# New places for the temporaries of the block products of q and k, and the forget gate's sums behind the second block unit

## The chip, the cores and the metric

The kernel runs on one core of one Trainium2 chip. The metric is the device time of one execution in microseconds. Engines: PE is TensorE (matmuls), DVE is VectorE, ACT is ScalarE, POOL is GpSimd, SP is SyncE, which here only issues DMAs.

## The reference

One decoder layer on 1024 tokens of width 1024, all in float32:

```python
h = rms_norm(x, norm_mix_g)
proj = h @ w_in                       # q, k, v of two attentions, forget gate, branch gates
f_logit = fox_gate_columns + b_fgt
# dilated sliding-window attention (3 groups of 4 heads)          -> o_a
# forgetting attention (8 heads): logits q.k/8 + sum of log f     -> o_b
o_b = forgetting_attention(q, k, v, log_sigmoid(f_logit))
merged = g_a * (o_a @ w_dil_out) + g_b * (o_b @ w_fox_out)
x = x + merged @ w_out
# then a SwiGLU feed-forward block and a last rms_norm
```

The change lies in the projections to q and k, and in the small computation that turns the forget gate's logits into running sums of their log sigmoids.

## The kernel before

Every float32 operand of a matmul is held as a pair hi and lo of the reduced type fp32r. `split` (L96, L97) makes the pair: ACT copies to hi, DVE subtracts to get lo. A product is three matmuls: hi by hi, hi by lo, lo by hi.

The stages around the change, in order:

- *Values.* After the norm and the transposes (`hT_t`), the values of the two attentions are projected. In the pool "dilv" this stage holds two staging tiles `vst` (2 KB per partition each, stored to `vd_dram` by ACT's DMA queue) and the weights `w12` (hi and lo, 16 KB each). Meanwhile `form` prepares T1 to T4, combinations of blocks of `hT_t`.
- *Block units for q and k.* `projections` computes two column blocks of 128 weights at a time by a Strassen-like scheme: seven products of 12 matmuls (L287) with combined weights and combined inputs in place of eight. There are nine such units: four for the forgetting attention (the outer loop's `pr` of 0 and 2, q and k each), five for the dilated one. `left_side` prepares the weights of a unit: two raw tiles are loaded by SP (L254), POOL adds and subtracts them in four operations (L275 to L280) into `s` tiles, and `split` makes `A1`, `S12`, `S34` and `A22`. Then `prod` and the evacuations alternate: `cc` is the first bank copied by ACT (L313), `v2`, `v3` and the outputs `qo` come from joins on DVE (L318, L320). For the forgetting attention each output is split once more (`qh`) and hi and lo are stored to `fqk_dram`; for the dilated one `qo` is stored to `dqk_dram` from POOL's queue (L306).
- *The gate's sums.* `decay` takes the gate's logits `lf` through exp, Ln and a few small DVE operations (L520 to L530), two small matmuls with triangular and full ones (L534, L535), and DVE operations on their result (`tot`, `negc`). `negc` is first read by the logits of the attention.
- *Attention.* Score matmuls (L634, L635), ACT takes them out of the banks with `negc` as bias into the tiles `L` (L638), POOL masks the diagonal blocks (L641), DVE takes maxima, POOL reduces them over partitions (L649), DVE subtracts (L662), ACT takes the exp (L668). Beside it run two more plain projections (`ahead`, `pf` banks), to fill TensorE.

On each engine the order is that of a planner, which takes the program's order, the dependences and its own costs; `tc.issue_after(x)` puts the instructions of a block behind `x` on the engine of `x`, with no wait of its own.

Memory per partition is a stack of pools. The pool "proj" of the block units and, after it, the pool "attention" start at the place where "dilv" started. Within a pool, tiles lie in the order in which they are first asked for, a tag with as many places as it has buffers. With `reuse_waits="tile"` a tile waits for what still uses the earlier tiles at its place. In "proj" the gate's five tiles are asked for first, then the tiles of `projections` as they come. In "attention" come first

```python
R0 = apool.tile([P, 256], F32, name="R0", bufs=1)
R1 = apool.tile([P, 2, 256], F32, name="R1", bufs=1)
R2 = apool.tile([P, P], F32, name="R2", bufs=1)
```

(1, 2 and 0.5 KB), then the two `L` tiles of the first half of the queries (5 KB each).

Of the kernel before, what the change touches and what calls it, by code (L numbers as in the profile page):

```python
# [8 lines left out]
F32 = mybir.dt.float32  # L9
# [38 lines left out]
def layer_kernel(  # L48
# [53 lines left out]
        last_mm[0] = nc.tensor.matmul(psum, w.lo, m.hi, start=False, stop=stop)  # L102

    last_mm, last_hi, last_sq = [None], [None], [None]
    last_w = [None]

    def load_w(src, kt, n, tag="w", bufs=2, pool=None, chunk=None, rpool=None, rbufs=2, shared=0, between=None):

# [151 lines left out]
        split(w.hi[:], w.lo[:], raw)  # L260
        return w

    def left_side(pool, rg, ru, bufs, a22_bufs=2):
# [11 lines left out]
        nc.gpsimd.tensor_tensor(out=s12[:, :4], in0=u1, in1=u2, op=ALU.add)  # L275
        nc.gpsimd.tensor_tensor(out=s12[:, 4:], in0=s12[:, :4], in1=g1, op=ALU.subtract)  # L276
        S12 = fill(pair(KT, "s12", bufs), s12[:])
        s34 = pool.tile([P, KT, P], F32, tag="s", name=nm("s34"), bufs=2)
        nc.gpsimd.tensor_tensor(out=s34[:, :4], in0=g1, in1=u1, op=ALU.subtract)
        nc.gpsimd.tensor_tensor(out=s34[:, 4:], in0=g2, in1=s12[:, 4:], op=ALU.subtract)  # L280
        return A1, S12, fill(S34, s34[:]), fill(A22, u2)

    def prod(bank, a, b, first=False):
        for k in range(4):
# [2 lines left out]
                last_mm[0] = nc.tensor.matmul(bank[:], p, q, start=first and k == 0 and n == 0,  # L287
                                              stop=k == 3 and n == 2, skip_group_check=True)

    def projections(pool, T, c, dst, dls, sc, hl=False):  # L290

        T1, T2, T3, T4 = T

        def put(i, hh, op):

            st = pool.tile([P, dls[i], HALF // dls[i]], F32, tag="qo", name=nm("qo"), bufs=4)
            op(st[:], dls[i])
            if hl:
                flat = st[:].rearrange("p r i -> p (r i)")
                hi = pool.tile([P, HALF], F32R, tag="qh", name=nm("qh"), bufs=2)  # L300
                split(hi[:], flat, flat)
                d = dst[i][:, :, hh * HALF:(hh + 1) * HALF]
                nc.scalar.dma_start(out=d[0], in_=hi[:].bitcast(F32))
                nc.gpsimd.dma_start(out=d[1], in_=flat)
            else:
                nc.gpsimd.dma_start(out=residues(dst[i], dls[i], hh), in_=st[:])  # L306

        cc, v2, v3 = [pool.tile([P, HALF], F32, tag=n, name=nm(n), bufs=1) for n in ("cc", "v2", "v3")]
        A1, S12, S34, A22 = left_side(pool, *[raw_w(w_in[:, c0:c0 + P]) for c0 in c], 1)
        b1, b2, b3 = pd(), pd(), pd()  # L310

        def copy(out, bank, r=1):
            nc.scalar.activation(out=out, in_=view(bank[:], r), func=AF.Copy, scale=sc)  # L313

        def join(out, bank, other, r=1):
            p, q = view(bank[:], r), view(other[:], r)
            if sc == 1.0:
                nc.vector.tensor_tensor(out=out, in0=p, in1=q, op=ALU.add)  # L318
            else:
                nc.vector.scalar_tensor_tensor(out=out, in0=p, scalar=sc, in1=q, op0=ALU.mult, op1=ALU.add)  # L320

        flat = view(cc[:], 1), view(v2[:], 1), view(v3[:], 1)
        prod(b1, A1[:, :4], B11, True)
        copy(flat[0], b1)
        prod(b2, S12[:, 4:], T2, True)
        join(flat[1], b2, cc)
        prod(b1, A1[:, 4:], B21)
        put(0, 0, lambda o, r: copy(o, b1, r))
        prod(b2, S34[:, :4], T3)
        join(flat[2], b2, cc)  # L330
        prod(b3, S12[:, :4], T1, True)
        put(1, 1, lambda o, r: join(o, b3, v3, r))
# [179 lines left out]

    def decay(sums, az, u, t1, tot):

        nc.gpsimd.memset(sums[:], 1.0)
        nc.gpsimd.affine_select(out=sums[:, 0], in_=sums[:, 0], compare_op=ALU.is_ge, fill=0.0, base=0,
                                pattern=[[1, P]], channel_multiplier=-1)

        z = lf[:].rearrange("p a b -> p (a b)")
        nc.vector.tensor_scalar(out=t1[:], in0=z, scalar1=-1.0, scalar2=None, op0=ALU.mult)  # L520
        nc.vector.tensor_tensor(out=az[:], in0=z, in1=t1[:], op=ALU.min)
        nc.scalar.activation(out=az[:], in_=az[:], func=AF.Exp)
        nc.vector.tensor_scalar(out=u[:], in0=az[:], scalar1=1.0, scalar2=None, op0=ALU.add)
        nc.vector.tensor_scalar(out=t1[:], in0=u[:], scalar1=-1.0, scalar2=None, op0=ALU.add)
        nc.vector.tensor_tensor(out=az[:], in0=az[:], in1=t1[:], op=ALU.subtract)
# [18 lines left out]


    with pool_of("proj", 1) as upool:
        cums = [upool.tile([P] + d, F32, name=n, bufs=1) for n, d in (
            ("sums", [2, P]), ("az", [NT * 8]), ("u", [NT * 8]), ("t1", [NT * 8]), ("tot", [NT, 8]))]
        for pr in range(0, 4, 2):
            for a in range(2):  # L550
                c0 = FOX0 + a * FOX_W + pr * P
                projections(upool, T, (c0, c0 + P), [fqk_dram[a, pr + i] for i in range(2)], (1, 1),
                            (SCALE, 1.0)[a], True)
            if pr == 0:
                decay(*cums)
        for two in TWOS:
# [737 lines left out]
```

## Time and profile before

| | us |
|---|---|
| median of 3 runs (lowest to highest) | 1478.67 (1477.41 to 1481.15) |
| span of the profiled execution | 1476.9 |
| TensorE busy in it | 1442.2 |
| VectorE, ScalarE, GpSimd busy | 956.6, 558.0, 488.5 |
| granted TensorE clock, mean | 0.995 of full speed |

The profile is of one execution. Its span runs from the first to the last instruction; of its own time no more than that span is given, and it lies 1.8 us under the median of the runs. Timeline rows give start and duration in microseconds, engine, line, operation, output and inputs, their sizes, a count of merged instructions, and in brackets the idle time of the engine just before and what ended it. Rows of waits give the total, the number of times and the longest. A row of a DMA gives size and median time from issue to landing. `wh` and `wl` name all hi and lo weight tiles of the units, also `S12`; `s` is a tile of combined weights. Some matmul records can be missing from a trace.

### The profile page before, as it was taken

What the parts mean: (1) busy time and instruction counts of PE and PEld (TensorE: products, weight loads), DVE (VectorE), ACT (ScalarE), POOL (GpSimd) and SP (SyncE); (2) the same over time, 40 slices, a digit from 0 to 9 for tenths busy, and PEclk for the clock granted to TensorE, in tenths of its full rate; (3) what the DMA queues carried; (4) which work ended last, traced back from release to release, by engine and by line L of the source; (5) the groups of instructions that cost most, each with busy time, mean ns of one, the idle gap of its engine ahead of it and who ended that gap; (6) DMA issues with size and microseconds to landing.
All of it is one profiled execution on the core that took longest, in us unless ns stands there. A gap on an engine that the chain in (4) does not pass through costs nothing.

```text
span 1476.9 us, 18419 instructions
## 1 busy us (share of the span) xinstructions
PE 1442.2 (98%) x6876; PEld 1160.9 (79%) x6876; DVE 956.6 (65%) x1344; ACT 558.0 (38%) x832; POOL 488.5 (33%) x438
## 2 busy tenths in 40 slices
PE   8999999999999999999999989999999999999997
PEld 7897888787676676788888778888888887788886
DVE  6482654449889899836627865555566554876556
ACT  5342332236556423354315332232223323533333
POOL 1002434435433221110146146666666665000000
PEclk9999999999999999999999999999999999999999
DMA  8232444474534461275859232232333334976602
GB/s 229 72 107 71 147 160 126 131 214 123 134 108 114 154 209 43 65 240 160 305 199 341 101 86 79 93 106 95 107 107 107 105 104 135 326 250 214 183 31 100
DMA packets 165785, 213.58 MB, mean 145 GB/s; under 512 B 13760, under 2 KB 115136, under 8 KB 165440
## 3 DMA queue, kind: packets, MB, share of 16 engines
q1 hardware_dynamic: 129376, 119.06, 26.4%
q0 software_dynamic: 15200, 55.07, 10.5%
q10 hardware_dynamic: 21120, 38.28, 8.2%
q8 instruction: 54, 0.88, 0.3%
q14 instruction: 35, 0.29, 0.1%
HBM read 146.32 MB, written 66.06 MB: 144 GB/s over the span
## 4 chain that ended last, share of the span: by engine, by line
PE 79%; DVE 12%; issue 3%; ACT 2%; POOL 2%; DMA 1%; SPq 1%; DVEq 0%; POOLq 0%; ACTq 0%
PE pd L287 33%; PE pd L1211 10%; PE pd L100 6%; PE pd L102 6%; PE pd L101 6%; PE pf L102 3%; PE pf L100 3%; PE pf L101 3%; PE pd L197 2%; PE pd L193 2%; PE pd L194 2%; DVE wl L97 2%; PE pd L685 1%; DVE f L1120 1%; ACT wh L96 1%
## 5 line engine op out<-in xcount | busy, mean ns | idle before, releaser
L287 PE MATMUL pd<-hT_t,wh 128*128 128x512 f32 x856 | 264.9, 391 | 2.4 <-ACT cc L313 0.8
L287 PE MATMUL pd<-tT,wh 128*128 128x512 f32 x768 | 236.1, 389 | 4.0 <-ACT wh L96 4.0
L97 DVE TENSOR_TENSOR wl<-wr,wh 128x1024 fp32r<-128x1024 f32 (+2 forms) x110 | 130.7, 1189 | 134.4 <-ACT wh L96 134.2
L96 ACT ACTIVATE wh<-wr 128x1024 fp32r<-128x1024 f32 (+2 forms) x110 | 95.5, 868 | 277.9 <-PE pd L287 163.5
L287 PEld LDWEIGHTS pd<-hT_t,wh 128*128 128x128 f32 x856 | 159.9, 188 | 39.4 <-DVE sg L1011 4.2
L287 PEld LDWEIGHTS pd<-tT,wh 128*128 128x128 f32 x768 | 144.0, 188 | 34.7 <-ACT wh L96 4.9
L287 PE MATMUL pd<-hT_t,wl 128*128 128x512 f32 x428 | 166.6, 389 | 0.0
L287 PE MATMUL pd<-tT,wl 128*128 128x512 f32 x384 | 148.5, 390 | 0.1
L100 PE MATMUL pf<-hT_t,wh 128*128 128x512 f32 x288 | 114.2, 397 | 1.0 <-ACT wh L96 1.0
L102 PE MATMUL pf<-hT_t,wl 128*128 128x512 f32 x288 | 114.2, 397 | 0.0
L101 PE MATMUL pf<-hT_t,wh 128*128 128x512 f32 x288 | 114.1, 396 | 0.0
L96 ACT ACTIVATE wh<-s 128x1024 fp32r<-128x1024 f32 x58 | 61.5, 1060 | 117.5 <-POOL s L276 87.1
L97 DVE TENSOR_TENSOR ol<-raw,oh 128x1024 fp32r<-128x1024 f32 x64 | 77.3, 1224 | 43.7 <-ACT oh L96 40.3
L275 POOL TENSOR_TENSOR s<-wr 128x512 f32<-128x512 f32 x29 | 56.6, 1951 | 142.5 <-PE pd L101 65.0
L96 ACT ACTIVATE oh<-raw 128x1024 fp32r<-128x1024 f32 x64 | 67.2, 1068 | 91.9 <-PE pd L1211 83.5
L287 PEld LDWEIGHTS pd<-hT_t,wl 128*128 128x128 f32 x428 | 80.4, 188 | 16.7
L97 DVE TENSOR_TENSOR wl<-s,wh 128x1024 fp32r<-128x1024 f32 x58 | 75.4, 1299 | 24.1 <-ACT wh L96 24.0
L1211 PE MATMUL pd<-ol,oh 128*128 128x512 f32 x224 | 87.2, 389 | 0.0
L1211 PE MATMUL pd<-oh,ol 128*128 128x512 f32 x224 | 86.2, 389 | 0.0
L1211 PE MATMUL pd<-oh 128*128 128x512 f32 x224 | 85.2, 390 | 0.7 <-DVE acc L1182 0.7
L958 POOL TENSOR_TENSOR r<-r 128x512 f32<-128x512 f32 x32 | 43.1, 1359 | 124.9 <-DMA r<-in_w_ffn_down_dram 123.6
L287 PEld LDWEIGHTS pd<-tT,wl 128*128 128x128 f32 x384 | 72.1, 188 | 15.3 <-DVE wl L97 0.5
(278 smaller groups left out, 3065.0 us busy)
## 6 DMA issues: line engine op xcount, KB each, us to landing
wr<-in_w_in_dram SPq DMA_DIRECT2D x46, 512.0 KB, 4.4
wr<-in_w_ffn_in_dram SPq DMA_DIRECT2D x44, 512.0 KB, 3.9
raw<-left_dram SPq DMA_DIRECT2D x56, 256.0 KB, 3.9
g_dram<-fst ACTq DMA_DIRECT2D x32, 256.0 KB, 2.4
land<-g_dram SPq DMA_DIRECT2D x16, 512.0 KB, 3.5
r<-in_w_ffn_down_dram SPq DMA_DIRECT2D x8, 1024.0 KB, 10.7
right_dram<-r POOLq DMA_DIRECT2D x8, 1024.0 KB, 5.9
left_dram<-f POOLq DMA_DIRECT2D x8, 1024.0 KB, 4.7
```

Source lines behind the costliest of these rows:

```text
L96: last_hi[0] = nc.scalar.activation(out=hi, in_=src, func=AF.Copy)
L97: return nc.vector.tensor_tensor(out=lo, in0=src, in1=hi.bitcast(F32), op=ALU.subtract)
L100: nc.tensor.matmul(psum, w.hi, m.hi, start=start, stop=False)
L101: nc.tensor.matmul(psum, w.hi, m.lo, start=False, stop=False)
L102: last_mm[0] = nc.tensor.matmul(psum, w.lo, m.hi, start=False, stop=stop)
L193: nc.tensor.matmul(pt[hh][:], w.hi[:, k], m.hi, start=(k == 0), stop=False)
L194: nc.tensor.matmul(pt[hh][:], w.hi[:, k], m.lo, start=False, stop=False)
L197: nc.tensor.matmul(pt[hh][:], w.lo[:, k], m.hi, start=False, stop=(k == kt - 1))
L275: nc.gpsimd.tensor_tensor(out=s12[:, :4], in0=u1, in1=u2, op=ALU.add)
L287: last_mm[0] = nc.tensor.matmul(bank[:], p, q, start=first and k == 0 and n == 0, stop=k == 3 and n == 2, skip_group_check=True)
L958: nc.gpsimd.tensor_tensor(out=out, in0=p, in1=q, op=ALU.subtract)
L1211: nc.tensor.matmul(bank[:], p, q, start=new and n == 0 and i == 0, stop=n == last and i == 2, skip_group_check=True)
```

## The change

Three things:

1. `reserve` asks for tiles only to fix their places. In "proj" the output tiles `qo` and `qh` now come first, then the gate's tiles, then `cc`, `v2`, `v3`, `s34` and `a22`; `s` and `s12` follow as they are first used.
2. In the first unit alone, the splits of `S34` and `A22` and the copy to `cc` are put behind the hi half of `S12` on ACT.
3. In `decay`, the memset of `sums` is put behind the latest unit's last sum on POOL, and the exp behind the latest hi split on ACT. `decay` is called once, after the second unit, so these are the second unit's.

```diff
+    def reserve(pool, *places):
+        for tag, shape, dtype, bufs in places:
+            for _ in range(bufs):
+                pool.tile([P] + shape, dtype, tag=tag, name=nm(tag), bufs=bufs)
+
...
         S12 = fill(pair(KT, "s12", bufs), s12[:])
+        s12_hi[0] = last_hi[0]
...
-        nc.gpsimd.tensor_tensor(out=s34[:, 4:], in0=g2, in1=s12[:, 4:], op=ALU.subtract)
-        return A1, S12, fill(S34, s34[:]), fill(A22, u2)
+        last_s[0] = nc.gpsimd.tensor_tensor(out=s34[:, 4:], in0=g2, in1=s12[:, 4:], op=ALU.subtract)
+        with tc.issue_after(s12_hi[0].ins) if first else ExitStack():
+            return A1, S12, fill(S34, s34[:]), fill(A22, u2)
...
         prod(b1, A1[:, :4], B11, True)
-        copy(flat[0], b1)
+        with tc.issue_after(s12_hi[0].ins) if first else ExitStack():
+            copy(flat[0], b1)
...
-        nc.gpsimd.memset(sums[:], 1.0)
+        with tc.issue_after(last_s[0].ins):
+            nc.gpsimd.memset(sums[:], 1.0)
...
-        nc.scalar.activation(out=az[:], in_=az[:], func=AF.Exp)
+        with tc.issue_after(last_hi[0].ins):
+            nc.scalar.activation(out=az[:], in_=az[:], func=AF.Exp)
...
     with pool_of("proj", 1) as upool:
+        reserve(upool, ("qo", [HALF], F32, 4), ("qh", [HALF], F32R, 2))
         cums = [upool.tile([P] + d, F32, name=n, bufs=1) for n, d in (
             ("sums", [2, P]), ("az", [NT * 8]), ("u", [NT * 8]), ("t1", [NT * 8]), ("tot", [NT, 8]))]
+        reserve(upool, *[(t, [HALF], F32, 1) for t in ("cc", "v2", "v3")],
+                *[("s34" + n, [KT, P], F32R, 1) for n in "hl"], *[("a22" + n, [4, P], F32R, 2) for n in "hl"])
...
             projections(upool, T, (c0, c0 + P), [fqk_dram[a, pr + i] for i in range(2)], (1, 1),
-                            (SCALE, 1.0)[a], True)
+                            (SCALE, 1.0)[a], True, pr + a == 0)
```

More of the change, by code (lines that the diff above doesn't have):

```diff
@@ L104, in layer_kernel @@
     last_mm, last_hi, last_sq = [None], [None], [None]
-    last_w = [None]
+    last_w, last_s, s12_hi = [None], [None], [None]
     def load_w(src, kt, n, tag="w", bufs=2, pool=None, chunk=None, rpool=None, rbufs=2, shared=0, between=None):
@@ L261, in pair_of, with left_side @@
         return w
-    def left_side(pool, rg, ru, bufs, a22_bufs=2):
+    def reserve(pool, *places):
+        for tag, shape, dtype, bufs in places:
+            for _ in range(bufs):
+                pool.tile([P] + shape, dtype, tag=tag, name=nm(tag), bufs=bufs)
+    def left_side(pool, rg, ru, bufs, a22_bufs=2, first=False):
         def pair(k, tag, bufs):
@@ L288, in prod, with projections @@
                                               stop=k == 3 and n == 2, skip_group_check=True)
-    def projections(pool, T, c, dst, dls, sc, hl=False):
+    def projections(pool, T, c, dst, dls, sc, hl=False, first=False):
         T1, T2, T3, T4 = T
@@ L308, in projections @@
         cc, v2, v3 = [pool.tile([P, HALF], F32, tag=n, name=nm(n), bufs=1) for n in ("cc", "v2", "v3")]
-        A1, S12, S34, A22 = left_side(pool, *[raw_w(w_in[:, c0:c0 + P]) for c0 in c], 1)
+        A1, S12, S34, A22 = left_side(pool, *[raw_w(w_in[:, c0:c0 + P]) for c0 in c], 1, 2, first)
         b1, b2, b3 = pd(), pd(), pd()
```

## The prediction

> **What bounds the kernel now.** I read the page's busy shares first: they say which engine the sum has to be made on.
>
> ```profile
> span 1476.9 us, 18419 instructions
> PE 1442.2 (98%) x6876; PEld 1160.9 (79%) x6876; DVE 956.6 (65%) x1344; ACT 558.0 (38%) x832; POOL 488.5 (33%) x438
> ```
>
> TensorE is busy 1442.2 of 1476.9 us. Whatever takes no matmuls away, and this change takes none, can at best win back some of the other 34.7 us. So the next view is the waits of TensorE alone, for the stretch from just before the first block unit to the start of attention (118 to 330 us), and after it the busy time by stage:
>
> ```profile
> PE pd L287 <- ACT wh L96: 1.0, 1, 1.0
> PE pd L287 <- ACT cc L313: 0.8, 1, 0.8
> ...
> 133.50:154.00 20.50, 18.60 (x82) 14.50 (x81) 14.04 (x16) 8.83 (x13) 12.92 (x11) 1.00 0.44 129
> 154.00:173.00 19.00, 19.00 (x85) 15.72 (x85) 13.06 (x22) 6.94 (x10) 8.10 (x7) 1.00 0.42 132
> 173.00:192.00 19.00, 19.00 (x85) 15.73 (x85) 10.68 (x13) 6.21 (x10) 7.56 (x8) 1.00 0.47 154
> ```
>
> The columns are length, then busy us of PE, PEld, DVE, ACT and POOL, then the granted clock. Only the first unit has holes; the next two run without one. The two holes in the order of time (start, duration, what, idle before it):
>
> ```profile
> 133.08 0.39 PE L101 MATMUL pd<-wv,hT_t 128*128 128x512 f32 x1
> 133.31 0.39 PE L102 MATMUL pd<-wv,hT_t 128*128 128x512 f32 x1
> ...
> 136.03 0.39 PE L287 MATMUL pd<-hT_t,wl 128*128 128x512 f32 x1
> 137.23 0.73 PE L287 MATMUL pd<-hT_t,wh 128*128 128x512 f32 x2 [0.81 <-ACT cc L313]
> 137.80 0.40 PE L287 MATMUL pd<-hT_t,wl 128*128 128x512 f32 x1
> ...
> 139.86 0.39 PE L287 MATMUL pd<-hT_t,wl 128*128 128x512 f32 x1
> 141.27 1.19 PE L287 MATMUL pd<-tT,wh 128*128 128x512 f32 x4 [1.02 <-ACT wh L96]
> ...
> 142.87 0.63 PE L287 MATMUL pd<-tT,wh 128*128 128x512 f32 x2
> ```
>
> What stands behind each is in the chain of waits and in the other engines' timelines:
>
> ```profile
> 133.47 0.24 PE pd L102
> 133.74 0.61 ACT vst L501
> 134.36 2.14 DMA vd_dram<-vst
> ...
> 134.78 0.63 ACT L96 ACTIVATE wh<-wr 128x512 fp32r<-128x512 f32 x1 [0.44 <-ACT vst L501]
> 136.58 0.60 ACT L313 ACTIVATE cc<-pd 128x512 f32<-128x512 f32 x1 [1.17 <-DMA vd_dram<-vst]
> 137.08 0.25 ACT L522 ACTIVATE az<-az 128x64 f32<-128x64 f32 x1
> 140.18 1.04 ACT L96 ACTIVATE wh<-s 128x1024 fp32r<-128x1024 f32 x1
> ...
> 133.57 1.28 POOL L275 TENSOR_TENSOR s<-wr 128x512 f32<-128x512 f32 x1 [65.04 <-PE pd L101]
> 138.02 1.30 POOL L280 TENSOR_TENSOR s<-wr,s 128x512 f32<-128x512 f32 x1
> ...
> 79.65 2.35 SPq L254 DMA_DIRECT2D wr<-in_w_in_dram  x2
> ```
>
> The first hole: TensorE reuses the bank of the first product and needs `cc` copied out of it; that copy waits for the last store of `vst`, under which `cc` lies. The second: the hi half of `S12`. Its weights were ordered at 79.65 us, but POOL stood idle 65.04 us until TensorE let go of the memory of `s`, and then ACT took the forget gate's exp (137.08) and Ln before the split at 140.18.
>
> **The change part by part.**
>
> *The new places.* Sizes from the code, in KB from the pool's start: the value stage before it holds `vst` at 0-2 and 2-4, `w12` hi at 4-20 and lo at 20-36; beyond 36 nothing of that stage lies. Before: the gate's tiles 0-2, `cc` 2-4, `v2`, `v3` 4-8, `s34` 8-16, `a22` 16-24, `s` 24-32, `s12` 32-40, `qo` 40-48, `qh` 48-52. The two waits above fit it: `cc` on a `vst`, `s` on `w12`. After: `qo` 0-8, `qh` 8-12, the gate's tiles 12-14, `cc` 14-16, `v2`, `v3` 16-20, `s34` 20-28, `a22` 28-36, `s` 36-44, `s12` 44-52. So POOL's four sums and `S12`'s two splits need nothing of the value stage and can run once the weights are in, long before 133 us. DVE idles 20.58 us ahead of 131.29 us and takes the lo half there:
>
> ```profile
> 131.29 0.20 DVE L520 TENSOR_SCALAR t<-lf 128x64 f32<-128x64 f32 x1 [20.58 <-DMA vd_dram<-vst]
> ```
>
> `s34`, `a22` and `cc` still lie under `w12`, free at 133.7; ACT then has its `vst` copy (to 134.36), one split of 1.04 and one of 0.63, and the copy to `cc` at 136.3, when the first product ends. With `S12` ready, the program's own order can hold: 12 matmuls of `S12` with T2 (2.7 us at 0.227 each, the distance of the starts at 133.08, 133.31 and on to 136.03) cover that copy of 0.60.
>
> *Its gain.* Hole one: the stream would go on at 136.03 + 0.23 = 136.26, and starts at 137.23; the first three matmuls after it take 0.81 in place of 0.68. Together 1.10. Hole two: 139.86 + 0.23 = 140.09 to 141.27 is 1.18, and to 142.87 1.60 us where six matmuls take 1.36, so 0.24 more. Together 1.42, and the sum 2.5 us. Bounds: 1.8 (the two idle times alone, 0.81 + 1.02) and 2.8 (if the row x4 and its neighbour are five matmuls and none is missing). If the plan keeps the second product of the same bank right behind the first, some 0.7 of hole one stays (`cc` from 136.3 in place of 136.58). I take 2.5.
>
> *The gate's sums.* The exp now follows the last `qh` split of the second unit, the memset the second unit's last sum:
>
> ```profile
> 150.31 1.31 POOL L280 TENSOR_TENSOR s<-wr,s 128x512 f32<-128x512 f32 x1
> 163.86 0.61 ACT L96 ACTIVATE qh<-qo 128x512 fp32r<-128x512 f32 x1
> ...
> 138.13 1.27 DVE L525 TENSOR_TENSOR az<-az,t 128x64 f32<-128x64 f32 x1
> 140.61 0.23 DVE L530 SCALAR_TENSOR_TENSOR lf<-lf,az 128x64 f32<-128x64 f32 x1
> 153.53 0.33 PE L534 MATMUL pd<-lf,sums 128*128 128x64 f32 x2
> ```
>
> From exp (137.08) to L530's end is 3.8 us, now in the third unit, whose 19 us hold 10.68 us of DVE and 6.21 of ACT: there is room, and TensorE runs there without a hole. What is queued behind: on ACT the third unit's splits behind the exp of 0.25 us and a Ln like it, on DVE its splits and joins, on POOL the memset and the mask of `sums`, on TensorE all matmuls behind L534, which waited 12.7 us past its data before. What DVE makes of its result, `tot` and `negc`, moves along and is first read at 321.70. Price: 0 if L534 again stands late enough, up to 3.8 if it is placed the whole chain too early. I take 0. No DMA is added or moved past another. On SP's queue the second unit's weight loads follow the first unit's last reads of their two buffers, POOL's sums among them, and so come earlier, if at all changed.
>
> *The far end of the pool.* This is where I see a cost. Attention's first tiles lie over this pool: `R0`, `R1`, `R2` at 0-3.5 and the first logits `L` at 3.5-8.5. Before, that `L` lay over `v2`, and ACT waited for the last join that reads it; after, it lies over the last `qo`, and must wait until that is stored.
>
> ```profile
> 320.52 1.06 DVE L320 SCALAR_TENSOR_TENSOR qo<-pd,v 128x512 f32<-128x512 f32 x1 [1.57 <-PE pd L287]
> 321.70 2.95 ACT L638 ACTIVATE L<-pd,negc 128x512 f32<-128x512 f32 x6 [5.74 <-DVE qo L320]
> 321.88 0.90 POOL L306 DMA_DIRECT2D dqk_dram<-qo  x1 [1.75 <-DVE dl L598]
> dqk_dram<-qo POOLq DMA_DIRECT2D x1, 256.0 KB, 4.3
> DMA to landing us min/median/max: 3.0/4.3/7.3
> ...
> 325.95 0.39 PE L100 MATMUL pf<-hT_t,wh 128*128 128x512 f32 x1
> 326.48 0.58 POOL L641 TENSOR_SCALAR_AFFINE_SELECT L<-L 128x128 f32<-128x128 f32 x2
> 333.37 1.80 POOL L649 PARTITION_ALL_REDUCE mx<-mx  x1 [6.31 <-issue]
> 337.27 0.50 PE L634 MATMUL pd<-qx,kx 128*128 128x512 f32 x1 [1.48 <-ACT L L638]
> ```
>
> That store, issued at 321.88, lands 4.3 us later, at 326.2 (the row of landings is that of the five `qo` stores issued between 300 and 325 us). So the first L638 starts 4.5 us later than now. Six of them take 2.95 us, so they end at 329.2 where they ended at 324.65. POOL's masks ended at 327.06, 2.4 us behind them, since POOL makes the tables `R` in between; it can now do that while it waits, and ends one mask (0.29) behind, at 329.5. The all-reduce starts 6.31 us after that, at 335.8 where it was 333.37: 2.4 us later. TensorE has matmuls of the next projection to fill in, but already stands 1.48 us at 337.27 for the logits that ACT can't take before the exp of that all-reduce; what is late there is late in the end. Cost 2.4. Bounds: 0, if the plan puts other logits ahead on ACT so that TensorE finds work, and 4.5, if the whole delay passes through.
>
> [...]
>
> *Sum.* 1476.9 - 2.5 + 2.4 = 1476.8 us of span, a tenth under now. The profiled execution's span lies 1.8 under the median of the runs, 1478.67, and near their lowest, 1477.41; on the median's scale I say 1478.5. About 0.3% (4.4 us) is what a measurement of this kernel can tell from no change: its own three runs spread 3.7.
>
> **The rivals.**
>
> *The late store is hidden* (chance 0.27). The instruction order is planned; if the plan sees the store it can give ACT the second head's logits first (their memory, 8.5-13.5, was left long ago) and TensorE the 48 matmuls of the next projection. For it: those matmuls stand right behind, at 325.95. Against: the all-reduce of the first head still waits. Time: 1478.67 - 2.5, up to 0.5 of remaining cost: 1476.5.
>
> *Slower, by the late store* (0.16). The stores of that stretch are slow, up to 7.3 us. With a landing of L from issue, the first logits start L + 0.2 late; if the masks shrink no gap, that passes through whole. From L = 2.3 on, passed through whole, the gain of 2.5 is eaten; at 4.3 the kernel ends at 1478.67 - 2.5 + 4.5 = 1480.7, and at 7.3 at 1483.7. Against: the 2.4 us by which POOL now trails ACT are room for it.
>
> *The gate's matmuls stall TensorE* (0.06). L534 placed at the third unit's start would hold the queue up to 3.8 us; with the far end's 2.4 the time is up to 1482.4. Against: 12.7 us of margin before.
>
> *It doesn't do what it says* (0.05). If the plan still starts the first unit with two products of one bank and a late split, 1.8 us or so stay, and with 2.4 at the far end the time is 1480.4.
>
> *More than the holes* (0.06). With the late store hidden, a shifted plan could also take ACT's logits ahead of the exp and so close the 1.48 us at 337.27: 1478.67 - 2.8 - 1.5 = 1474.4, and less if others of TensorE's 34.7 us close too. Against: nothing in the edit aims there.
>
> **How the numbers follow.** The forecast has 0.40. Faster by over 0.3% (below 1474.2) needs the last rival with the scatter of the runs, and a little of the hidden store: 0.11. Slower (above 1483.1) needs the slow store passed through whole, or two costs together: 0.09. Within 0.3%: 0.80. The range reaches from a little under the hidden store with its best gain (1478.67 - 2.8 = 1475.9), less the 1.5 of the last rival and a little scatter, 1474, to the slow store at L near 6.5, 1483. The likeliest's own range, with the gain 1.8 to 2.8 and the cost a us to either side, 1.4 to 3.4, is 1477.3 to 1480.3.
>
> **What would show it.** Right: POOL's first L275 and `S12`'s split start before 120 us; TensorE's waits for `cc` and `wh` in the first unit are gone and its stream from 133.5 to 154 us is 2.5 us shorter; L522 comes after 160 us with no wait of TensorE at L534; the first L638 waits for a DMA of `qo` and TensorE's idle time near 337 us grows by what the all-reduce comes later. Wrong: no DMA named at L638 (the places at the far end are not as I worked out), a wait at L534, or holes between units where there were none.

## The result, and the profile after

| | before | after |
|---|---|---|
| median of 5 runs each, us | 1481.15 | 1496.97 |
| span of the profiled execution, us | 1476.9 | 1495.1 |
| granted TensorE clock, mean | 0.995 | 0.988 |

After over before is 1.0123, 95% interval 1.0108 to 1.0138. The changed kernel is slower by 1.23%, some 18 us, as are the profiled spans (18.2). The medians shown differ by 15.8 us: the ratio is not their quotient (1.0107). It is what the means give if only the three runs shown ahead count for the kernel before; with all five the means give 1.0111. The forecast was no change, with 1483 as its upper end, and it was wrong.

The same busy shares as before:

```profile
span 1495.1 us, 18414 instructions
PE 1451.3 (97%) x6876; PEld 1167.1 (78%) x6876; DVE 962.1 (64%) x1344; ACT 556.6 (37%) x832; POOL 494.5 (33%) x438
```

TensorE has the same 6876 matmuls, but 9.1 us more busy time and 9.1 us more idle time (43.8 for 34.7). Most of the idle part is in its waits from 118 to 350 us, in the new program's lines:

```profile
PE pd L544 <- DVE lf L540: 9.6, 1, 9.6
PE pd L647 <- ACT L L651: 3.3, 1, 3.3
PE pd L294 <- DVE v L325: 0.8, 1, 0.8
```

L544 is the first of the gate's two matmuls (L534 before), L647 and L651 are the score matmul and the logits (L634 and L638 before), L294 the unit matmul (L287 before). The first unit's two waits of before, 0.8 us for `cc` and 1.0 for `wh`, are gone; one of 0.36 for a `wh` stands at its last product. One wait of 9.6 us is new. The engines' timelines around it, first TensorE, then ACT, then DVE:

```profile
174.83 0.62 PE L294 MATMUL pd<-hT_t,wh 128*128 128x512 f32 x2
175.28 0.39 PE L294 MATMUL pd<-hT_t,wl 128*128 128x512 f32 x1
185.23 0.66 PE L544 MATMUL pd<-lf,sums 128*128 128x64 f32 x2 [9.56 <-DVE lf L540]
...
186.08 1.20 PE L294 MATMUL pd<-hT_t,wh 128*128 128x512 f32 x2
...
190.98 0.62 PE L294 MATMUL pd<-tT,wh 128*128 128x512 f32 x2
...
179.30 0.63 ACT L96 ACTIVATE qh<-qo 128x512 fp32r<-128x512 f32 x1 [1.53 <-DVE qo L325]
179.84 0.24 ACT L532 ACTIVATE az<-az 128x64 f32<-128x64 f32 x1
...
178.59 0.68 DVE L325 TENSOR_TENSOR qo<-pd,v 128x512 f32<-128x512 f32 x1
...
180.93 1.25 DVE L533 TENSOR_SCALAR u<-az 128x64 f32<-128x64 f32 x1
182.21 1.19 DVE L534 TENSOR_SCALAR t<-u 128x64 f32<-128x64 f32 x1
...
184.86 0.22 DVE L540 SCALAR_TENSOR_TENSOR lf<-lf,az 128x64 f32<-128x64 f32 x1
```

The gate's matmuls stand directly behind the last product of the second unit, which ends at 175.67. The exp stands behind the split of an output that is joined from that same product (join 178.59, split 179.30, exp 179.84), and `lf` comes 5.2 us after the exp starts. So TensorE waits 4.2 us for the exp to start and 5.2 for the chain behind it, with all later matmuls queued behind it.

Much of the added busy time is the clock. The 12 unit matmuls from 186.08 to 190.98 take 4.90 us, at full speed 2.72 (12 at 0.227, the distance of the starts at clock 1.00). The busy time by stretches says it too (length, busy us of PE, PEld, DVE, ACT, POOL, then the clock, the DMA share and GB/s):

```profile
180.00:185.00 5.00, 0.00 (x0) 0.00 (x0) 4.72 (x9) 0.34 (x2) 3.35 (x3) 0.53 0.63 198
185.00:190.00 5.00, 4.77 (x13) 4.00 (x14) 1.56 (x10) 0.00 (x0) 0.00 (x0) 0.50 0.62 169
190.00:195.00 5.00, 5.00 (x22) 4.07 (x21) 0.69 (x1) 0.60 (x1) 0.00 (x0) 0.95 0.00 0
```

The granted clock fell to half there (0.53, then 0.50). By the shares in the rows this began at 180.3 us, 4.6 us after the last matmul, and ended at 190.5, 5.3 us after the first one behind the gap.

Read in finer stretches, the clock in the traces is 1.00 or 0.50, nothing between, and outside the kernel's start and end each stretch at 0.50 lasts 3.4, 6.8 or 10.2 us. Before has one of 6.8 us between 100 and 1465 us (at 557.8); after has 10.2 at 180.3, 6.8 at 337.3 and 3.4 at 569.4 and 883.4. As an estimate, with half of TensorE's busy time inside these stretches lost, and the kernel's start counted, that is 11.5 us after and 5.1 before: 6.4 of the 9.1 us of added busy time.

The far end shows the wait that the prediction named there. In order: POOL's store and all-reduce, ACT's first logits, DVE's table, TensorE:

```profile
334.18 0.72 POOL L313 DMA_DIRECT2D dqk_dram<-qo  x1 [1.76 <-DVE dl L611]
349.05 1.80 POOL L662 PARTITION_ALL_REDUCE mx<-mx  x1 [6.18 <-issue]
...
338.44 2.83 ACT L651 ACTIVATE L<-pd,negc 128x512 f32<-128x512 f32 x6 [10.18 <-DMA dqk_dram<-qo]
...
337.35 0.43 DVE L617 CAST R<-dl 128x512 f32<-128x512 int32 x1 [2.87 <-DMA dqk_dram<-qo]
...
332.86 0.47 PE L647 MATMUL pd<-qx,kx 128*128 128x512 f32 x1
339.18 0.58 PE L647 MATMUL pd<-qx,kx 128*128 128x256 f32 x1 [3.32 <-ACT L L651]
353.98 0.50 PE L647 MATMUL pd<-qx,kx 128*128 128x512 f32 x1 [0.20 <-ACT L L651]
361.89 1.51 PE L698 MATMUL pd<-L,v 128*64 128x128 f32 x12
```

ACT waits for the store issued at 334.18 and starts 4.3 us later. TensorE's wait of before, 1.48 us some 16.4 us behind the first score matmul (337.27 - 320.85), is now 0.20 (at 353.98, 21.1 us behind it). The 3.32 us are a new wait, 6.3 us behind the first score matmul, for a bank that ACT has not yet emptied. From 337.3 on TensorE runs at half clock for 6.8 us, which before did not do there at all.

As a ledger, after minus before in the profiled executions, each a distance to the one event above it: the first unit starts 0.95 us later (the instructions of TensorE up to there are the same, so this is no part of the change; near 15 us this execution has 6.8 us at half clock and the one of before 3.4); its first 60 matmuls take 2.7 us less; from there to the first score matmul (320.85 before, 332.86 after) 13.7 us are lost, nearly all at the gate's matmuls; from there to the first values (345.42, 361.89) 4.5; to the end another 1.8.

### The profile page after: what moved, and what is told of

It is laid out like the page before. It is cut to its first block, busy times and chain, and to the rows that moved or that the text cites. A ratio compares the mean times of both kernels' runs of the same rounds, so it can differ in the third digit from the quotient of the medians.

```text
span 1495.1 us, 18414 instructions
## 1 busy us (share of the span) xinstructions
PE 1451.3 (97%) x6876; PEld 1167.1 (78%) x6876; DVE 962.1 (64%) x1344; ACT 556.6 (37%) x832; POOL 494.5 (33%) x438
## 4 chain that ended last, share of the span: by engine, by line
PE 78%; DVE 11%; DMA 4%; issue 2%; ACT 2%; POOL 2%; ACTq 0%; SPq 0%; DVEq 0%; POOLq 0%
PE pd L294 32%; PE pd L1224 10%; PE pd L100 5%; PE pd L101 5%; PE pd L102 5%; PE pf L102 3%; PE pf L100 3%; PE pf L101 3%; DVE wl L97 2%; PE pd L698 2%; PE pd L197 2%; PE pd L194 2%; PE pd L193 2%; DMA wr<-in_w_in_dram 1%; PE pd L647 1%
## 5 line engine op out<-in xcount | busy, mean ns | idle before, releaser
L294 PE MATMUL pd<-hT_t,wh 128*128 128x512 f32 x856 | 267.8, 395 | 1.6 <-ACT c L1093 0.7
L294 PE MATMUL pd<-tT,wh 128*128 128x512 f32 x768 | 235.6, 390 | 3.1 <-ACT wh L96 2.3
L294 PEld LDWEIGHTS pd<-hT_t,wh 128*128 128x128 f32 x856 | 161.9, 190 | 38.8 <-DVE sg L1024 4.2
L294 PEld LDWEIGHTS pd<-tT,wh 128*128 128x128 f32 x768 | 144.0, 188 | 34.1 <-ACT wh L96 3.1
L294 PE MATMUL pd<-hT_t,wl 128*128 128x512 f32 x428 | 167.8, 392 | 0.0
L294 PE MATMUL pd<-tT,wl 128*128 128x512 f32 x384 | 148.2, 390 | 0.5 <-DVE wl L97 0.5
L294 PEld LDWEIGHTS pd<-hT_t,wl 128*128 128x128 f32 x428 | 81.1, 190 | 17.1
L294 PEld LDWEIGHTS pd<-tT,wl 128*128 128x128 f32 x384 | 72.1, 188 | 16.2 <-DVE wl L97 1.4
```

## The experiments

Each is the changed kernel with one edit, unless it says otherwise. Ratios are against the kernel before, timed in the same session. The last three columns are changes of a distance against before, in us, from the profiled executions: "unit 1" from the first unit's first matmul to its 61st, "units" from there to the first score matmul, "far end" from there to the first values. "Half clock" is the time in the far end at which the granted clock was 0.50; before has none there. The profiles are of one execution each, so these columns hold whatever the clock did in it.

| kernel | ratio | 95% interval | unit 1 | units | far end | half clock |
|---|---|---|---|---|---|---|
| as changed | 1.0123 | 1.0108 to 1.0138 | -2.7 | +13.7 | +4.5 | 6.8 |
| no_gate_edges | 1.0057 | 1.0042 to 1.0073 | +0.5 | -0.6 | +4.7 | 6.8 |
| far_end_moved | 1.0105 | 1.0085 to 1.0125 | -2.7 | +13.3 | +2.1 | 3.4 |
| both | 1.0025 | 1.0013 to 1.0036 | +0.5 | -0.6 | +2.0 | 3.4 |
| gate_edges_alone | 1.0094 | 1.0076 to 1.0113 | -0.5 | +12.5 | +1.8 | 3.4 |
| warm_wait | 1.0095 | 1.0081 to 1.0110 | -2.7 | +11.4 | +6.2 | 6.8 |
| late_matmuls | 1.0045 | 1.0027 to 1.0062 | -2.7 | +5.6 | +2.6 | 3.4 |
| late_far | 1.0020 | 1.0010 to 1.0029 | -2.7 | +5.7 | -0.4 | 3.4 |
| mid_far | 1.0030 | 1.0017 to 1.0044 | -2.7 | +5.0 | 0.0 | 0 |
| gate_first | 1.0070 | 1.0058 to 1.0083 | -0.8 | -1.9 | +2.0 | 3.4 |
| gate_first_no_edges | 1.0045 | 1.0032 to 1.0059 | -0.1 | -2.0 | +2.1 | 3.4 |
| gate_split | 1.0012 | 1.0001 to 1.0022 | -1.2 | -0.6 | +1.0 | 0 |
| gate_split_ne | 1.0002 | 0.9990 to 1.0013 | -0.7 | -0.3 | +0.1 | 0 |
| gate_early | 1.0004 | 0.9995 to 1.0013 | -2.7 | +0.2 | +1.5 | 3.4 |
| gate_early_ne | 0.9991 | 0.9979 to 1.0003 | -0.7 | -0.3 | 0.0 | 0 |

### The two suspects, apart and together

no_gate_edges takes the two edges of `decay` away:

```diff
-        with tc.issue_after(last_s[0].ins):
-            nc.gpsimd.memset(sums[:], 1.0)
+        nc.gpsimd.memset(sums[:], 1.0)
...
-        with tc.issue_after(last_hi[0].ins):
-            nc.scalar.activation(out=az[:], in_=az[:], func=AF.Exp)
+        nc.scalar.activation(out=az[:], in_=az[:], func=AF.Exp)
```

> The change without its two edges in decay (memset behind the second unit's last sum, exp behind its last hi split); the new places and the first unit's edges stay. Theory, the gate's matmuls stand right behind the second unit's last product while exp waits for that product's own split: TensorE's wait of 9.6 us for lf and the slow matmuls behind it (some 2.4) go, so about 12 us under the changed kernel, some 5 to 6 over the kernel before (the wait for the stored qo stays). Rival, the new places disturb the second unit's loads and the edges only show it: within 2 us of the changed kernel.

far_end_moved asks for other tiles first in "attention", so that those that are written late lie where `qo` was:

```diff
+        reserve(apool, ("o", [HALF], F32, 2), ("den", [HALF], F32, 1), ("rc", [HALF], F32, 1))
```

> The change with attention's late tiles (o, den, rc, 8 KB) reserved first, so that they and not the tables R and the first logits L lie over qo. Theory: the first L651 no longer waits for the store of qo, TensorE's 3.3 us at its third-last score of the first group and the slow matmuls behind it (2.2) go: 5 to 6 us under the changed kernel, 12 to 13 over the kernel before. Rival, attention makes the delay up later (TensorE then waits elsewhere, at the all-reduce): under 2 us of difference.

The kernel "both" has both edits.

> Both of the above: no gate edges and attention's late tiles first. Theory: what stays is the first unit's gain, measured as 2.7 us in the changed kernel, so 1 to 4 us under the kernel before, ratio 0.997 to 0.999. Rival, the places cost something else in the units as well: at or over the kernel before.

gate_edges_alone is the kernel before with nothing but `decay`'s two edges:

```diff
+        with tc.issue_after(last_s[0].ins):
+            nc.gpsimd.memset(sums[:], 1.0)
...
+        with tc.issue_after(last_hi[0].ins):
+            nc.scalar.activation(out=az[:], in_=az[:], func=AF.Exp)
```

> The kernel before with the two edges of decay alone, old places, nothing at the first unit. Theory: the same wait at the gate's matmuls, 8 to 10 us and 2.4 of slow matmuls, so 10 to 13 us over the kernel before, less the part of the first unit's holes that exp and Ln made (under 1). Rival, places: within 2 us of the kernel before.

Measured: without the edges 1486.11 us where before is 1477.94, with the tiles moved 1492.45, with both 1482.15. All three fell short of their theory: no_gate_edges is 8.2 us over before and not 5 to 6, far_end_moved wins some 3 us on the changed kernel by the ratios and not 5 to 6, and "both" lies over before, where its rival had put it. Alone on the kernel before, the edges cost 1.0094, and TensorE's waits (118 to 350 us; the gate's lines of the kernel before have moved by 2) show the same number:

```profile
PE pd L536 <- DVE lf L532: 9.6, 1, 9.6
```

So the two edges of `decay` are the greater loss by themselves, with none of the new places. Without them, though, the first unit's gain goes as well. The waits of no_gate_edges:

```profile
PE pd L294 <- ACT wh L96: 3.0, 2, 2.8
```

With the gate's exp back in the first unit ACT comes to a split 2.8 us too late. The gain and the loss hang on the same edge: what is cleared out of the first unit has to go elsewhere.

At the far end the place of `qo` is worth 4.46 - 2.07 = 2.4 us with the edges and 4.65 - 2.01 = 2.6 without. Some 2 us remain, which gate_edges_alone (1.84) has too, with no new places; the last column says where most of them go. The far ends of far_end_moved, "both" and gate_edges_alone each hold 3.4 us at half clock, in which TensorE is busy for 3.0 to 3.4 us and so loses 1.5 to 1.7 by the estimate used above. mid_far, with the tiles moved and no half clock there, loses 0.0. And of the 2.4 to 2.6 for the place, some 1 us is the second 3.4 us at half clock and 0.9 to 1.2 idle time.

### The wait without the cold clock

warm_wait puts 33 small matmuls of constants, whose result is not used, behind the second unit's last product, ahead of the gate's matmuls:

```diff
+        for _ in range(33):
+            with tc.issue_after(last_mm[0].ins):
+                nc.tensor.matmul(pc[:, 128:256], ones[:], ones[:], start=True, stop=True)
```

> The changed kernel with 33 idle matmuls (ones by ones, 0.28 us each, 9.2 us in all, into the free part of the same bank) right ahead of the gate's two, so that TensorE is busy while lf is late; lf comes no earlier. Theory, the idle time itself lowers the granted clock: the clock stays at 1.00 between 175 and 195 us, the 12 matmuls behind the gate's take 2.7 in place of 4.9 us, and the kernel is about 2 us faster than the changed one. Rival, the slow matmuls have another cause (late weights): same time as the changed kernel or slower.

Its stretch from 180 us, where the changed kernel has 0.53:

```profile
180.00:185.00 5.00, 3.55 (x28) 3.06 (x27) 3.91 (x10) 0.26 (x1) 2.55 (x3) 1.00 0.63 171
```

The clock stays at 1.00 (a wait of 1.45 us for `lf` is left), and the first score matmul comes 2.3 us sooner than in the changed kernel (+11.4 for +13.7); the 12 unit matmuls behind the gap, slowed from 2.72 to 4.90 us, had said 2.2. So some 2.3 us of the loss are the clock, the rest the wait. At the far end this kernel loses 1.8 us more than the changed one, so its ratio doesn't show the 2.3 by itself.

### Giving the chain more time

late_matmuls moves the gate's matmuls and what follows them behind the third unit, late_far moves the tiles at the far end as well. mid_far puts the exp behind the first unit's last hi split, with the tiles moved:

```diff
+                if pr == 2 and a == 0:
+                    decay_sums(*cums)
```

```diff
-        with tc.issue_after(last_hi[0].ins):
+        with tc.issue_after(after_hi.ins):
...
+                if pr == 0 and a == 0:
+                    unit1_hi = last_hi[0]
```

> The change with the gate's two matmuls and what follows them (tot, negc) called one unit later, behind the third unit; the exp stays behind the second unit's last split. Theory, the stall is the place of the two matmuls in TensorE's queue: lf is ready some 10 us before they are reached, the wait of 9.6 us and the slow matmuls are gone and the first unit keeps its gain of 2.7: 11 to 14 us under the changed kernel, 2 to 5 over the kernel before (the far end's wait stays). Rival, it is the gate's small operations, late on ACT and DVE, that hold up the next unit's splits wherever the matmuls stand: a wait of several us for wh or wl in the third unit, under 6 us won.

> The late matmuls, and attention's late tiles reserved first. Theory: the first unit's gain without either cost: 1 to 4 us under the kernel before, ratio 0.997 to 0.999. Rival, the gain is given back in attention, as the kernel with both edges out and the tiles moved did: within 1 us of the kernel before or over it.

> The change with the exp behind the first unit's last split instead of the second's (the matmuls stay behind the second unit in the program), and attention's late tiles first. Theory: lf is ready near 170 us, before the second unit's last product ends at 175.7, so no wait at the gate's matmuls, while the first unit keeps its gain: 1 to 4 us under the kernel before. Rival, the exp's place matters less than its lateness anywhere behind the first unit: a wait for lf of over 2 us stays.

The 9.6 us are gone in all three, but none reaches the kernel before, and 5.0 to 5.7 us are still lost in the units. TensorE's waits in late_matmuls, and then its DVE and POOL:

```profile
PE pd L294 <- DVE v L327: 2.4, 1, 2.4
...
184.09 1.29 DVE L533 TENSOR_SCALAR u<-az 128x64 f32<-128x64 f32 x1
185.41 1.21 DVE L534 TENSOR_SCALAR t<-u 128x64 f32<-128x64 f32 x1
...
188.06 0.68 DVE L327 SCALAR_TENSOR_TENSOR v<-pd,cc 128x512 f32<-128x512 f32 x1
...
183.66 1.67 POOL L285 TENSOR_TENSOR s<-wr,wr 128x512 f32<-128x512 f32 x1 [1.95 <-DVE wl L97]
185.29 1.28 POOL L286 TENSOR_TENSOR s<-wr,s 128x512 f32<-128x512 f32 x1
```

The gate's small operations now stand on DVE ahead of the joins (`v`) that TensorE needs, and hold them by 2.4 us (2.7 in mid_far). Each of the first two ends with an addition of POOL (183.66 + 1.67 = 185.33, 185.29 + 1.28 = 186.57). The clock falls after that too, for 3.4 us from 189.6 on:

```profile
189.70:192.90 3.20, 3.20 (x9) 2.51 (x8) 1.92 (x2) 1.50 (x2) 0.54 (x1) 0.50 1.10 391
```

That costs another 1.7 us by the same estimate, behind a wait of 2.4 that ended at 188.8; the changed kernel's was 9.6. What lowers the clock isn't shown here. The wait and the clock are 4.1 of the 5.6 us; a wait of 1.9 us for the load of `qx`, just ahead of the first score matmul (0.4 before), is most of the rest.

### The gate's work ahead of the units

gate_first calls `decay` ahead of the first unit, without its two edges, with its temporaries past 36 KB and `sums` and `tot` at the pool's start; `qo` moves to 27 to 35 KB, away from the far end's tiles. gate_first_no_edges also drops the first unit's edges.

```diff
+        sums = upool.tile([P, 2, P], F32, name="sums", bufs=1)
+        tot = upool.tile([P, NT, 8], F32, name="tot", bufs=1)
+        reserve(upool, ("qh", [HALF], F32R, 2), ...
+        reserve(upool, ("qo", [HALF], F32, 4), ("pad", [192], F32, 1), ("s", [KT, P], F32, 2),
...
+        decay(sums, az, u, t1, tot)
...
-            if pr == 0:
-                decay(*cums)
```

> The gate's sums ahead of all block units instead of behind two of them: decay is called before the loop, its three small tiles lie behind everything the value stage still uses, sums over the earlier vst, its edges are gone. qo lies at 27-35 KB, so the tables and the first logits of attention no longer lie over it. The first unit's edges stay. Theory: the gate's small operations run in the stretch where DVE and ACT stand idle (111 to 131 us) and cost nothing there; the first unit keeps its 2.7 us, there is no hole in the second and third unit and no wait for the store of qo: 1 to 4 us under the kernel before, ratio 0.997 to 0.999. Rival, the first unit's gain is always paid back in attention: within 1 us of the kernel before or over it.

> The same without the first unit's two edges (copy to cc and the splits of S34 and A22 behind the hi half of S12). Theory: with the gate out of the way and S12 ready early the edges bind nothing, so the same time within 1 us and no new hole in the first unit. Rival, they are what keeps the order of ACT right: a wait for cc or wh of 1 us or more comes back in the first unit.

```profile
PE pd L542 <- POOL sums L524: 7.6, 1, 7.6
...
131.77 0.31 POOL L523 MEMSET sums<- 128x256 f32 x1 [62.76 <-DMA vd_dram<-vst]
138.96 1.25 POOL L280 TENSOR_TENSOR s<-wr 128x512 f32<-128x512 f32 x1 [6.88 <-issue]
```

`sums` lay over a `vst`, so its memset waited until 131.77, and on POOL everything stands behind it, the first unit's sums too. Then POOL's first addition came 6.88 us late with no releaser named, and TensorE stood 7.6 us for `sums`, ahead of the first unit, which began at 142.61 us and had 3.9 us at half clock in it. That was a fault of this experiment's places, not an answer. gate_first_no_edges has the same stall (8.2 us), and no wait came back in its first unit. It was expected within 1 us of gate_first and came out 4.05 us faster; in the profiles that lies behind the first values, and its cause isn't shown.

gate_split keeps these places but leaves the memset (with its edge), the mask, the matmuls and what follows them (`decay_sums`) behind the second unit; only exp to `lf` come first, without an edge. gate_split_ne drops the first unit's edges.

```diff
+        decay(az, u, t1)
...
             if pr == 0:
-                decay(*cums)
+                decay_sums(sums, tot)
```

> The gate's elementwise work (exp to lf) is done ahead of the first unit, in memory past 36 KB, where its inputs don't wait for the value stage; its memset, mask, matmuls, tot and negc stand behind the second unit, with none of the two edges of the changed kernel; qh, v2, v3 and not qo lie under attention's first tiles. My theory (what is lost is lost by the gate's small operations between TensorE's joins and by an idle TensorE that then runs at a lower granted clock, and the far end's loss is the place of qo): no wait of TensorE for lf or sums of more than 0.5 us, no wait of the first logits for a store of qo, the first unit's stream 2.0 to 2.8 us shorter than before, and a ratio of 0.998 to 1.000 (1475.5 to 1478.5 us where before is 1478.7). Rival one, that the first unit's gain is always given back by the units behind it, whatever the gate does, because their weights, sums and splits are no earlier: a ratio of 1.000 to 1.002, with the gain seen at the 60th unit matmul and gone at the 120th. Rival two, that ACT's exp and Ln ahead of the first unit delay the copies of the value stage and so the start of the first unit: the start is 0.5 to 1.5 us later and the ratio 1.000 to 1.002.

> The same without the first unit's edges (splits of S34 and A22 and the copy of the first bank behind the hi half of S12). My theory: with the gate's work gone from the first unit the planner's own order serves, and the result is that of the kernel with those edges within 1 us, a ratio of 0.998 to 1.000. Rival: without those edges ACT takes a late split before an early one, TensorE waits up to 1.5 us for cc or wh in the first unit, and the ratio is 1.000 to 1.001.

No stall at the gate's matmuls, no wait for a store, and ratios of 1.0012 and 1.0002. But ACT's order in gate_split, with TensorE's wait:

```profile
138.43 1.20 PE L294 MATMUL pd<-tT,wh 128*128 128x512 f32 x4 [1.21 <-ACT wh L96]
...
135.58 0.26 ACT L526 ACTIVATE az<-az 128x64 f32<-128x64 f32 x1 [0.44 <-ACT vst L509]
137.18 0.26 ACT L532 ACTIVATE u<-u 128x64 f32<-128x64 f32 x1 [1.34 <-DVE t L530]
137.34 1.04 ACT L96 ACTIVATE wh<-s 128x1024 fp32r<-128x1024 f32 x1
```

The exp and the Ln still came behind the last copy of `vst` and ahead of the split, although their input had been ready 19 us. The theory expected 2.0 to 2.8 us at the first unit and got 1.2, and both ratios lie over the 0.998 to 1.000 expected.

gate_early therefore writes exp to `lf` into the value stage, between two copies of `vst`, over the weights `w0` that are no longer needed; gate_early_ne again drops the first unit's edges.

```diff
+                if (g0, tt) == (1, 5):
+                    w0_ctx.__exit__(None, None, None)
+                    with pool_of("gate", 1, side="right") as gpool:
+                        decay(*[gpool.tile([P, NT * 8], F32, name=n_, bufs=1) for n_ in ("az", "u", "t1")])
...
+        with tc.issue_after(last_st[0].ins):
+            nc.scalar.activation(out=az[:], in_=az[:], func=AF.Exp)
```

> As the kernel with the gate's work split, but the elementwise part (exp to lf) stands inside the value stage, between two copies of vst on ACT, in three small tiles over the weights that the value stage no longer needs; the sums and matmuls behind the second unit, the first unit's edges kept. My theory: what held the first unit's splits in that kernel (TensorE 1.21 us idle for the hi half of S12, behind exp and Ln on ACT at 135.58 and 137.18 us) is gone, the first unit's stream is 2.5 to 2.8 us shorter than before (distance from the first to the 60th unit matmul 13.6 to 13.9 us where it was 16.37), the gate's matmuls wait for nothing, and the ratio is 0.997 to 0.9995 (1474.2 to 1478.2 us where before is 1478.98). Rival: the gain is there at the 60th unit matmul, but the units behind it and the attention give it back, since their order is replanned and their waits are others; then no single wait over 1 us is named and the ratio is 1.000 to 1.002.

> The same without the first unit's edges. ACT then takes the copy of the first bank ahead of the hi half of S12. My theory: TensorE waits 0.5 to 0.9 us for cc in the first unit and 0 to 0.6 for a join behind it, so 0.7 to 1.5 us more than with the edges there, and the ratio is 0.998 to 1.000. Rival: the edges do nothing once the gate is out of the way; the first unit is within 0.3 us of that with them.

gate_early, the stretches of the first three units (the first of these rows starts 1 us ahead of the unit, which begins at 134.53); they answer to the three rows of before in the prediction:

```profile
133.50:154.00 20.50, 20.35 (x90) 16.32 (x89) 11.45 (x11) 8.52 (x12) 8.54 (x8) 1.00 0.39 115
154.00:173.00 19.00, 19.00 (x87) 15.71 (x86) 12.45 (x20) 7.13 (x10) 7.50 (x7) 1.00 0.42 136
173.00:192.00 19.00, 19.00 (x86) 15.73 (x85) 10.01 (x13) 7.02 (x10) 7.08 (x7) 1.00 0.47 159
```

Here is the whole gain: the first unit 2.7 us shorter, no wait of TensorE for a unit's data, and the first score matmul still 2.45 us closer to the first unit's start than before. Yet the time is 1478.74 us where before is 1478.07. gate_early_ne has two waits in the first unit:

```profile
137.13 0.74 PE L294 MATMUL pd<-hT_t,wh 128*128 128x512 f32 x2 [0.69 <-ACT cc L320]
149.27 0.74 PE L294 MATMUL pd<-tT,wh 128*128 128x512 f32 x2 [0.97 <-DVE v L327]
```

It reaches the first score matmul only 0.94 us sooner, 1.5 us behind gate_early, and ends ahead of it: 1476.52 us. It is the best kernel found, some 20 us faster than the changed one, but against before its interval (0.9979 to 1.0003) includes no difference. The two differ in the first unit's edges alone. Between the first score matmul and the end of the attention (the matmuls with `oh` and `wh`, at 649.5 us before) gate_early loses 1.2 us against before and gate_early_ne wins 1.9, with TensorE's instructions in another order there, though neither edits that part. So the rival of gate_early's expectation was right about the ratio and the place, though a wait of 2.2 us is named there and not none over 1 us. What the rival did not name is the clock. The far ends of the two, gate_early first:

```profile
319.40:345.48 26.08, 23.79 (x105) 19.47 (x105) 18.67 (x41) 17.20 (x37) 13.90 (x23) 0.93 0.61 154
319.94:344.46 24.52, 22.49 (x104) 18.08 (x104) 17.85 (x38) 15.46 (x34) 12.11 (x21) 1.00 0.58 147
```

From the first score matmul to the end of the attention, before has 6.8 us at half clock, gate_early 10.2 and gate_early_ne 3.4. Half of these times is 3.4, 5.1 and 1.7 us: 1.7 more and 1.7 less than before, where 1.2 more and 1.9 less were measured. All the runs together say the same. Their mean granted clock is 0.9950 before (21 runs), 0.9933 in gate_early and 0.9951 in gate_early_ne (11 each). As an estimate, (1 - clock) times the span is 7.4, 9.9 and 7.2 us. What is left of the span is 1469.1, 1467.1 and 1467.9 us, so gate_early is 2.0 under before there and gate_early_ne 1.2, near their gains at the first score matmul (2.45 and 0.94). So by this estimate the units' gain is kept to the end, and in gate_early the clock takes it back. Whether the new order brings the lower clock isn't shown.

## Why the prediction was wrong, by its own steps

*The gate's sums: the step that failed.* The prediction priced this part at 0, bounded it by 3.8 us, and gave a stall at L534 a chance of 0.06; it cost some 13 of the 18 us. Four things were wrong in it.

First, the row was misread. The split at 163.86 was taken for the second unit's last `qh` split and is the first unit's: products and evacuations of neighbouring units overlap. In the kernel before, `q` units are joined with a scale (L320) and `k` units without (L318); the first unit is `q`, the second `k`, and these are the last join of the first and the last join and split of the second:

```profile
163.06 0.69 DVE L320 SCALAR_TENSOR_TENSOR qo<-pd,v 128x512 f32<-128x512 f32 x1 [0.64 <-PE pd L287]
...
183.46 0.69 DVE L318 TENSOR_TENSOR qo<-pd,v 128x512 f32<-128x512 f32 x1 [0.64 <-PE pd L287]
...
184.20 0.62 ACT L96 ACTIVATE qh<-qo 128x512 fp32r<-128x512 f32 x1
```

So the exp moved 43 us, not 27, and not into a stretch of slack, but behind the second unit's last join.

Second, the margin belonged to the old order. L534 waited 12.7 us past its data before, and this was used as a cover. But the same edit moved the data, and nothing moved L534 as far: it stands behind the second unit's last product, whose own output the exp now has to wait for. In that order a wait is certain.

Third, the bound left out the way to the exp. From the product's end through join and split to the exp are 4.2 us, and the chain took 5.2 us in place of 3.8, two of its operations taking 1.2 us each. The upper bound should have been their sum, 8 us even with the old 3.8.

Fourth, the clock was not in the sum: 2.3 us by warm_wait.

*The new places.* Right in mechanism: POOL's four sums started at 91.26 us ("before 120 us" was said), released by the last matmul that reads `w0`. One statement of it was wrong: "beyond 36 nothing of that stage lies". `w0` lies there, from the other side of the memory:

```profile
91.26 1.93 POOL L280 TENSOR_TENSOR s<-wr 128x512 f32<-128x512 f32 x1 [21.79 <-PE pd L102]
```

The split of `S12` was put "before 120 us" too and came at 135.72, the first ACT work behind the last `vst` copy. It was in time all the same.

*Its gain.* Predicted 2.5 us, measured 2.7 between these two rows (149.90 in the kernel before, 0.95 us later start):

```profile
148.17 0.62 PE L294 MATMUL pd<-tT,wh 128*128 128x512 f32 x2
149.90 0.62 PE L287 MATMUL pd<-tT,wh 128*128 128x512 f32 x2
```

The bounds, 1.8 to 2.8, held it. The two waits that it named are gone, but for the 0.36 us at the unit's last product.

*The far end of the pool.* Right in the wait, lucky in its price. The logits waited for a store of `qo`, 4.3 us from issue to start against 4.3 from the row, and the place cost 2.4 to 2.6 us against 2.4, but not on the path that was priced. POOL was to make the tables `R` during the wait; they lie over `qo` too, and DVE's work on one of them waited for a store of `qo` (337.35). So the all-reduce came 16.2 us behind the first score matmul where it came 12.5: 3.7 later, not 2.4. The wait that was to grow with it fell from 1.48 to 0.20, and the cost came as the new wait of 3.32 for a bank and 6.8 us at half clock, neither of which the prediction had. The whole far end lost 4.5.

*The sum.* -2.7 and +2.4 would have left the kernel where it was, as forecast. Some 13 us of the error are the step put at 0, and the chances followed it; the far end adds 2.1 (4.5 for 2.4). Of "what would make the prediction wrong", "a wait at L534" is what came.

Open: what sets off the stretches at half clock in the far end, which are most of the 2.0 us that the place doesn't explain, and the 1.8 us that the changed kernel lost behind the first values.

## What to carry to other kernels

When an edge moves a chain of small operations, find its consumer in the new order of the consumer's engine, add up everything from what the edge follows to the consumer, and only then speak of margin; a margin read off the old order is worth nothing if the edit moves its other end. Price a TensorE wait of 2 us and more at its length plus the slow clock that may follow it (2.3 us behind the 9.6 here, by warm_wait). And before a gain or loss of 2 us far from the edit is put down to the edit or to a new order, read the granted clock there: one stretch of 3.4 us at half clock costs 1.7 us by the estimate used here, and a profile of one execution shows that execution's stretches.

## What the runs showed of the hardware

- The sixteen traces have 49 stretches at clock 0.50 between 100 and 1465 us: 34 of 3.4 us, 7 of 6.8 and 8 of 10.2. All but one begin within 4.7 us after the start of a TensorE gap of 1.6 us or more. But 19 gaps of 1.45 to 3.0 us had none begin in the 7 us behind them. A gap of 2.2 us that stands near 550 to 567 us in 14 of the traces was followed by 10.2 us at half clock in three, 6.8 in four, 3.4 in three and none in four. So the length of the gap doesn't decide it; what does isn't shown.
- DVE operations on 128x64 elements took 1.29 and 1.21 us in late_matmuls while POOL was adding weights (L285, L286); each ended within 0.05 us of one of POOL's additions (183.66 + 1.67 = 185.33 and 185.38; 185.29 + 1.28 = 186.57 and 186.62). With POOL idle, in gate_early, the same operations took 0.20 us each:

```profile
119.19 0.20 DVE L507 TENSOR_SCALAR u<-az 128x64 f32<-128x64 f32 x1 [3.18 <-ACT az L506]
119.42 0.20 DVE L508 TENSOR_SCALAR t<-u 128x64 f32<-128x64 f32 x1
```

  Why the slow ones end with POOL's additions isn't shown.
- POOL's first addition behind the memset in gate_first began 6.88 us after POOL was free, and the all-reduce of the changed kernel 6.18 us, both put down to issue. In both, POOL's queue has two instructions MODIFY_POOL_CONFIG directly ahead (132.10 and 343.07 us). In the kernel before, those ahead of the additions stand at 68.60, with 65 us of idle time behind them, and cost nothing; in gate_first the 6.88 us were most of TensorE's wait of 7.6 us. That these instructions took that time isn't shown.
